# Pads of 96 instead of 64 columns around the sort buffers of a graph scatter kernel

## The chip, the cores and the metric

The kernel runs on one core of a Trainium2 chip. The metric is the device time of one execution in microseconds (us). Ten runs of the kernel before gave a median of 493.8 us, from 493.12 to 495.82.

## What is computed

There are N = 4096 nodes with 256 features each and E = 262144 edges, each with a source and a destination node. Every node gets its own features times `w_self`, and for each edge that ends in it the source's features times `w_msg`:

```python
self_out = nodes @ w_self
msg = nodes[edges_src] @ w_msg
agg = np.zeros((N, D)); np.add.at(agg, edges_dst, msg)
return self_out + agg
```

## The kernel before, in words

**Two stages.** The kernel first sorts the edges by a key made of the destination's segment, the source's block and the two low parts (lines 146 to 182), and then counts and multiplies. For a run of sorted edges that share a source block and a destination segment, TensorE adds up a matrix of edge counts with one-hot matrices (`onehots`, `count_mm`, lines 308 to 359), ScalarE copies it out of PSUM (`evac`), GpSimd's queue merges overlapping parts by DMA (`merge`), and TensorE multiplies it by Y = nodes @ w_msg (`apply_run`). This main loop begins at about 195 us. It takes its keys from the sort, so it can't begin before the sort is done. All instructions are issued in an order written out by hand (`tc.manual_schedule()`, line 98): on each engine they run in the order of the code.

**The sort's data.** The 262144 keys lie as 128 partitions by 2048 columns of f32. There are two such buffers, `XA[0]` and `XA[1]`, and each pass reads one and writes the other. Each buffer has `FP` columns in front of the keys, set to a very low value, and `BP` = 128 columns behind them, set to a very high one (lines 160 to 162). `FP` was 64.

**The sort's passes.** `SORT_A` (line 39) is a list of steps. `('b', h, par)` is a pass of compare-exchanges along the columns with gap h: VectorE writes the minimum of column c and column c + h to c, and the maximum to c + h, one instruction each (`mm`, line 591, with line 593 in the profile). Blocks of b columns, where b is the lowest set bit of h, are paired, and `par` says whether the even or the odd blocks are the lower ones. Each gap comes as two passes, par 0 and 1. `('q', bb, rots)` is a rotation: each group of columns is shifted across the partitions by its own number of rows. `rotate` (line 706) does it in two halves of 1024 columns. A half is 8 matmuls in the code (16 records in the trace) with a shifted identity, into two PSUM tiles, each copied out by ScalarE (line 719) into the other buffer. `('sh', ...)` is a shuffle on VectorE.

The part of the list around the change, after the gaps 962, 239, 376, 283 and 203:

```python
('b', 119, 0), ('b', 119, 1), ('b', 87, 0), ('b', 87, 1),
('q', 32, [...]), ('b', 78, 0), ('b', 78, 1), ('b', 30, 0), ('b', 30, 1), ('b', 42, 0), ('b', 42, 1),
('q', 16, [...]), ('b', 22, 0), ('b', 22, 1), ('b', 29, 0),
```

**Two ways to do a pass.** `run` (line 724) chooses by the gap. A gap above `FP` goes to `far_gap` (line 668), which does both passes of that gap in seven instructions and touches only columns that have a partner inside the keys; its first instruction reads nearly all columns. Gaps up to `FP` that follow each other are taken together by `near` (line 643). There a pass runs from -h to 2048, so that columns at the edges have a partner in the pads and nothing is left over. `near` can cut passes in two:

- *behind* a rotation (its argument `behind`): the first two passes start with the columns that depend on the first 1024 alone, as a first wave;
- *ahead* of a rotation (`ahead`): the last two passes are done first up to the columns that make the first 1024 complete, and then the rest, as a last wave. The cuts move with the gap and the block (lines 649 to 659).

`passes` (line 629) issues the waves one after the other. If a rotation is ahead, `near` also calls `warm` (line 597): ten matmuls of 512 zero columns, whose start is tied to an instruction of VectorE that lies at least 4.2 us (`PE_WARM_UP`) before the last wave, by an estimate of each instruction's length (columns / 960 + 0.1 us, line 589). `far_gap` calls no `warm`.

**After these steps** more groups of `near` and rotations follow, then a last rotation that is also a transpose (line 767) into `XS`, a pass list along the other direction (`SORT_S`), and between them `project` (line 220), which computes Y on TensorE and ScalarE; it needs `XT`, which the SP queue loads with 64 transposing DMAs (line 212).

## Time and profile before

| | |
|---|---|
| median of 10 runs | 493.8 us |
| the profiled execution's own time | 493.15 us |
| mean granted TensorE clock of the records | 0.915 |
| TensorE (PE) busy | 351.1 us, 71% |
| VectorE (DVE) busy | 446.3 us, 91% |
| ScalarE (ACT) busy | 239.3 us, 49% |
| GpSimd (POOL) busy | 158.3 us, 32% |
| passes on XA, line 593, all groups | 152 instructions |

The profile is of one execution. In the page's row by slices (40 equal ones, the busy share in tenths) the two stages can be told apart: VectorE is busy in nearly all of them up to the last two, TensorE fully only from the middle on.

```profile
PE   0000560575575006799999999999999999899995
DVE  8999399999889999999999999999999999989810
PEclk9999967799789556599999999999999999999999
```

A slice is 12.3 us. The 3 in the fifth slice of VectorE's row (49 to 61 us) is where the changed steps lie. PEclk is the granted clock of TensorE in tenths of full speed, as far as its records go. PE is the matmul side of TensorE and PEld the weight loads, L593 a line of the kernel; a matmul of f32 appears as two records. The table of waits names who waited, for whom, the us in total, how often, and the longest.

### The profile page before, as it was taken

To read this page: it belongs to the slowest core of one execution; us is meant where nothing else is said; L and a number is where in the kernel's file an instruction comes from. 1 tells how busy PE (TensorE), PEld (TensorE's weight loads), DVE (VectorE), ACT (ScalarE), POOL (GpSimd) and SP (SyncE) were. 2 spreads that over 40 slices of the span, in tenths; PEclk is the share of its full clock that TensorE was granted. 3 is DMA by queue.
4 is the path that set the end of the run, shared out by engine and by line. 5 is a ranking of instruction groups with operands and counts; after the bars stand their busy time and mean duration, and the time that the engine had idled before them with its cause. 6 is when DMAs were issued, how large, how long until landed. Compare 5 with 4: busy or idle time off the path is not lost.

```text
span 491.3 us, 10292 instructions
## 1 busy us (share of the span) xinstructions
PE 351.1 (71%) x4012; PEld 309.6 (63%) x4017; DVE 446.3 (91%) x411; ACT 239.3 (49%) x452; POOL 158.3 (32%) x154
## 2 busy tenths in 40 slices
PE   0000560575575006799999999999999999899995
PEld 0000530353452003699999999999999999799984
DVE  8999399999889999999999999999999999989810
ACT  3100110021155003457777777777777776677762
POOL 9100000000000000136455555555546454545640
PEclk9999967799789556599999999999999999999999
DMA  8971111111000000123333433344433343424341
GB/s 327 177 200 25 25 27 25 26 25 22 2 0 1 0 0 2 8 21 25 46 39 38 46 40 43 37 45 40 46 37 45 36 50 30 49 29 50 34 45 44
DMA packets 57756, 22.20 MB, mean 45 GB/s; under 512 B 43882, under 2 KB 56682, under 8 KB 57706
## 3 DMA queue, kind: packets, MB, share of 16 engines
q0 software_dynamic: 35920, 8.91, 21.6%
q1 hardware_dynamic: 21210, 10.52, 7.9%
q10 hardware_dynamic: 576, 2.10, 1.1%
q8 instruction: 33, 0.54, 0.5%
q14 instruction: 17, 0.14, 0.1%
HBM read 8.92 MB, written 6.30 MB: 31 GB/s over the span
## 4 chain that ended last, share of the span: by engine, by line
DVE 36%; PE 35%; issue 13%; POOL 13%; ACT 2%; DMA 1%; POOLq 0%; ACTq 0%; DVEq 0%
DVE XA L593 19%; PE ring L340 15%; PE out_ps L407 13%; POOL atr L384 13%; DVE XS L593 9%; PE tp_sw L715 4%; PE out_ps L402 2%; DVE e_oh L315 1%; DVE lo_c L123 1%; DVE d_oh L315 1%; PE out_ps L396 1%; DMA atr<-atr 1%; DVE XS L260 1%; ACT XA L719 1%; DVE XA L180 1%
## 5 line engine op out<-in xcount | busy, mean ns | idle before, releaser
L384 POOL DMA_DIRECT2D atr<-atr x130 | 145.2, 1180 | 318.3 <-ACT atr L364 315.0
L364 ACT CAST atr<-ring 128x486 bf16<-128x486 f32 x352 | 193.3, 567 | 85.7 <-PE ring L340 72.6
L340 PE MATMUL ring<-d_oh,e_oh 128*128 128x112 bf16 x2048 | 195.9, 215 | 7.8 <-DVE d_oh L315 5.0
L340 PEld LDWEIGHTS <-e_oh 128*128 128x128 bf16 x2048 | 166.9, 99 | 17.8 <-issue 7.0
L407 PE MATMUL out_ps<-Y,atr 128*128 128x256 bf16 x1056 | 170.0, 272 | 0.1
L315 DVE TENSOR_TENSOR e_oh<-slo_b,jrow 128x4096 bf16<-128x4096 int16 (+2 forms) x68 | 146.7, 2157 | 10.7 <-PE ring L340 10.3
L315 DVE TENSOR_TENSOR d_oh<-rel_b,jrow 128x3584 bf16<-128x3584 int16 (+2 forms) x68 | 129.5, 1904 | 0.0
L593 DVE TENSOR_TENSOR XA<-XA 128x510 f32<-128x510 f32 (+35 forms) x136 | 92.1, 722 | 12.8 <-ACT XA L719 11.1
L407 PEld LDWEIGHTS <-atr 128*128 128x128 bf16 x1056 | 92.1, 97 | 7.0 <-DMA atr<-atr 0.4
L340 PE MATMUL ring<-zer 128*128 128x224 bf16 x352 | 92.2, 262 | 0.9 <-ACT vals L265 0.7
L715 PE MATMUL tp_sw<-XA,id 128*128 128x128 f32 x192 | 28.2, 310 | 56.7 <-DVE XA L593 56.7
L605 PE MATMUL warm<-zw 128*128 128x512 bf16 x65 | 23.5, 524 | 62.4 <-DVE XA L593 32.6
L715 PEld LDWEIGHTS tp_sw<-XA,id 128*128 128x128 f32 x192 | 26.8, 222 | 60.1 <-issue 58.5
L719 ACT COPY XA<-tp_sw 128x512 f32<-128x512 f32 x24 | 14.2, 591 | 101.1 <-PE tp_sw L715 101.1
L605 PEld LDWEIGHTS <-zw 128*128 128x128 bf16 x70 | 8.2, 124 | 74.6 <-DVE XS L593 29.4
L593 DVE TENSOR_TENSOR XS<-XS 128x512 f32<-128x512 f32 (+17 forms) x40 | 46.0, 1196 | 2.6 <-ACT XS L771 2.0
L340 PEld LDWEIGHTS <-zer 128*128 128x128 bf16 x352 | 34.5, 98 | 1.3 <-ACT o_sb L416 0.5
L402 PE MATMUL out_ps<-Y,atr 128*128 128x256 bf16 x123 | 33.4, 271 | 0.1
L265 ACT CAST vals<-tp_sw 128x512 int16<-128x512 f32 x4 | 2.3, 585 | 36.2 <-PE tp_sw L264 36.2
L593 DVE TENSOR_TENSOR XA<-XA,XA 128x62 f32<-128x62 f32 (+7 forms) x16 | 14.7, 918 | 0.3
L224 PE MATMUL y_ps<-wcat,XT 128*128 128x256 bf16 x64 | 10.5, 270 | 3.3 <-ACT Y L228 3.3
L402 PEld LDWEIGHTS <-atr 128*128 128x128 bf16 x123 | 11.9, 96 | 0.3
(85 smaller groups left out, 113.9 us busy)
## 6 DMA issues: line engine op xcount, KB each, us to landing
atr<-atr POOLq DMA_DIRECT2D x98, 56.0 KB, 2.8
out_dram<-o_sb SPq DMA_DIRECT2D x110, 32.0 KB, 1.5
s<-in_edges_src_dram ACTq DMA_DIRECT2D x4, 512.0 KB, 9.3
d<-in_edges_dst_dram SPq DMA_DIRECT2D x4, 512.0 KB, 5.3
nodes_bf<-in_nodes_dram POOLq DMA_DIRECT2D x1, 2048.0 KB, 16.5
nodes_bf_dram<-nodes_bf SPq DMA_DIRECT2D x1, 2048.0 KB, 8.7
XT<-nodes_bf_dram SPq DMA_TRANSPOSE x64, 2.4
atr<-atr POOLq DMA_DIRECT2D x32, 28.0 KB, 2.8
```

Of the source, the lines that this page charges most:

```text
L123: nc.vector.tensor_scalar(out=out, in0=in_, scalar1=float(lo), scalar2=float(hi), op0=ALU.max, op1=ALU.min)
L224: nc.tensor.matmul(out=y_ps[:], lhsT=XT[:, k, t * P:(t + 1) * P], rhs=wcat[:, 2 + k, :], start=(k == 0), stop=(k == 1),)
L315: tt(out=o[:, 0:n // 2], in0=val[:, c:c + n].rearrange("p (g i) -> p g i", i=2).unsqueeze(2).to_broadcast(shp), in1=jrow[:, 0:wid, :].unsq ...
L340: mm = nc.tensor.matmul(out=ap, lhsT=lhsT, rhs=rhs, start=start, stop=True, skip_group_check=True,).ins
L364: ins = nc.scalar.copy(out=at[:, 0:SW + W], in_=ring[:, b:b + SW + W]).ins
L384: nc.gpsimd.dma_start(out=atr[:, b:b + n, 0:W], in_=atr[:, a:a + n, SW:SW + W], accum_op=ALU.add)
L402: nc.tensor.matmul(out=out_ps[:, 0, :], lhsT=spill[:, SW:SW + P], rhs=Y[:, b, :], start=False, stop=False, skip_group_check=True,)
L407: nc.tensor.matmul(out=out_ps[:, t, :], lhsT=at[:, t * P:(t + 1) * P], rhs=Y[:, b, :], start=False, stop=(b == NB - 1), skip_group_check=True,
L593: self.nc.vector.tensor_tensor(out=out, in0=in0, in1=in1, op=op),
L605: ins = self.nc.tensor.matmul(out=w[:], lhsT=self.zw[:, 0:P], rhs=self.zw[:], start=True, stop=True).ins
L715: self.nc.tensor.matmul(out=tp[:, g * P:(g + 1) * P], lhsT=self.turned(rots[8 * h + 4 * t + g]), rhs=sel(x)[:, 4 * t + g], start=True, sto ...
L719: self.nc.scalar.copy(out=sel(y)[:, 4 * t:4 * t + 4], in_=tp[:].rearrange("p (g i b) -> p g i b", g=4, b=bb),)
```

## The change

One constant: the pads in front of the sort buffers are 96 columns wide instead of 64, and since `run` compares the gaps with the same constant, gaps up to 96 are taken by `near` instead of `far_gap`.

```diff
-FP = 64
+FP = 96
 BP = 128
```

Nothing else is edited. The gaps of the list between 65 and 96 are 87 and 78, each with two passes. Gap 87 becomes a group of its own with a rotation ahead and none behind; gap 78 joins the group of 30 and 42, which thereby has a rotation behind it as well as ahead.

## Prediction

> **What bounds the kernel now.** I read the page first: its span, and the chain that ended last by engine.

> ```profile
> span 491.3 us, 10292 instructions
> DVE 36%; PE 35%; issue 13%; POOL 13%; ACT 2%; DMA 1%; POOLq 0%; ACTq 0%; DVEq 0%
> ```

> The chain changes hands once: VectorE (DVE) carries the sort, TensorE and the merges the main loop behind it. The change touches only the sort, so the second view is the table of who waited for whom, VectorE alone.

> ```profile
> DVE XA L593 <- ACT XA L719: 11.1, 6, 7.3
> DVE e_oh L315 <- PE ring L340: 10.3, 7, 3.8
> ```

> Six waits of the sort for the copy that ends a rotation (L719) sum to 11.1 us, and one of them alone is 7.3. The other row (one-hots waiting for TensorE) lies, by the timeline, wholly after 391 us; from 57 to 391 us VectorE has no gap over 2 us. So a microsecond that the sort saves starts the main loop a microsecond earlier, and nothing else that could set the end stands still: the transposing loads of XT end at 120 us and `project`, which needs them, starts at 141.7.

> Third, where the 7.3 us lies: the chain in order of time, 44.7 to 76 us (start, length, what).

> ```profile
> 44.78 1.20 DVE XA L593
> ...
> 49.62 6.75 PE tp_sw L715 x32
> ...
> 56.40 0.59 ACT XA L719
> ...
> 57.02 1.20 DVE XA L593
> ...
> 62.06 2.40 DVE XA L593 x2
> ...
> 66.92 1.40 DVE XA L593 x2
> 68.33 1.35 DVE XA L593 x2
> ...
> 69.82 2.04 PE tp_sw L715 x16
> ...
> 71.88 0.59 ACT XA L719
> ...
> 72.50 1.30 DVE XA L593 x2
> ```

> Two rotations stand side by side here. The first, `('q', 32, ...)`, lies between the gaps 87 and 78, which go through `far_gap`: VectorE ends gap 87 at 49.71, all 32 matmul records run with nothing beside them, and VectorE resumes at 57.02. The second, `('q', 16, ...)`, lies between groups that `near` cuts: the chain holds only the first half of the rotation (x16), VectorE's other waves run beside it, and its gap is 72.16 to 72.50, 0.34 us. The change makes the first look like the second.

> Last, the rows of the stretches, with busy time, count and clock (columns PE, PEld, DVE, ACT, POOL, PEclk, DMA share, GB/s).

> ```profile
> 49.71:57.01 7.30, 6.65 (x32) 6.46 (x32) 0.00 (x0) 2.34 (x4) 0.00 (x0) 1.00 0.12 27
> 69.70:72.17 2.47, 2.02 (x16) 1.86 (x16) 2.43 (x4) 0.87 (x2) 0.00 (x0) 1.00 0.12 27
> L715 PE MATMUL tp_sw<-XA,id x64: 275/275/551, 49.6 to 74.1; 128*128 128x128 f32 x64
> ```

> Half a rotation takes 3.3 us in the first row and 2.0 in the second, though both rows say clock 1.00. The third row (min, median, max ns of a matmul) tells why: 551 is twice 275, so the first rotation ran on a half clock; the record of the clock simply has no entry before it. No `warm` precedes that rotation, because only `near` with a rotation ahead calls it.

> **The change part by part.** With FP = 96 the test `op[1] <= FP` takes in the gaps 87 and 78 and no others.

> *Gap 87* becomes a `near` of two passes, cut ahead of the rotation. By L643-664 the cuts are 1112 and 1024: wave 1 has min/max pairs of 599 and 556 columns, wave 2 pairs of 468 and 512; 4270 columns in 8 instructions for 3922 in 7. Prices from rows of `near`: 1040 columns take 1239 ns and 554 take 734, so 1.04 ns a column; a pair of 1038 takes 62.06 to 64.49 = 2.42 us, which leaves 0.26 us a pair. Then 4270 x 1.04 ns + 4 x 0.26 = 5.48 us against 4.93 now (44.78 to 49.71): +0.55.

> *Gap 78* joins the group 30, 42, cut behind the rotation at 944 and 864: pairs of 510 and 472, then of 552 and 592; 4252 columns for 3940. 4252 x 1.04 ns + 4 x 0.26 = 5.46 against 5.04 now (57.02 to 62.06): +0.42. The later passes of the group keep their cuts.

> *The rotation.* Wave 1 of gap 87 takes 2310 x 1.04 ns + 0.52 = 2.92, by its nearest row (2176 columns in 66.92 to 69.68) 2.76 + 134 x 1.04 ns = 2.90; I take 2.90: it ends at 47.68. At the second rotation the way from there to VectorE's restart is 69.68 to 72.50 = 2.82 (semaphore, 16 matmuls, two copies). Restart: 50.50. Wave 2 fills 2.58 of it, so a gap of 0.24 stays of 7.31. VectorE then has 1964 columns of gap 78 that need only the first half: 1964 x 1.04 ns + 0.52 = 2.56 us. At the second rotation the last copy ended 2.45 after the restart (74.37 + 0.58 - 72.50), so the second half is hidden, with 0.1 us in hand; if that is missed, the cost is what the copy is late.

> The sum: next group at 47.68 + 2.82 + 5.46 = 55.96 instead of 62.06, a gain of 6.10 us. The same from the terms: 7.31 - 0.24 - 0.55 - 0.42 = 6.10. What is late next is VectorE itself, which has no gap before the next rotation.

> *The added `warm`.* Ten matmuls on a TensorE that is idle then; they wait for an instruction of VectorE, and behind them stands only the rotation. Counting back 4.2 us by L589's estimates from the end of wave 1 (556, 556, 599, 599, 59, 59, 905: 4.17; so one more 905: 5.21) ties them to the 60-column max of gap 119, done at 42.33; start 42.48, as at the next warm-up 0.15 after. There ten took 4.43 us at half clock; here they end by 46.9, before 47.83, when the rotation can start. They delay nothing; whether they do their work is the open cost.

> [...] Row first: at the next warm-up, 64.60 to 69.03, the rows of one microsecond show the clock at 0.50 up to 69.0 and 0.79 in 69 to 70, so it rose at 69.42; it had fallen at 59.18 (0.59 in 59 to 60), 10.24 earlier. [...] I take the row: gain 6.1. [...]

> [...] Now one of them starts cold (VectorE's gap at 126.5 us is 1.94 instead of about 0.35) the others are warm. Bounds: all warm -1.6; one more fully cold +2.6. I take 0. [...]

> *Pads.* The memsets of 96 columns instead of 64 lie at 1.4 to 1.8 us on POOL; the 64-column one takes 0.17 us, so two of them cost under 0.2 us together on a queue whose nodes arrive long before use. VectorE's first dependent work is far later. Nothing. No DMA is added or moved.

> **The rivals.**

> *Cold rotation, or one later rotation cold.* Gain 3.5 to 4.4: 489.4 to 490.3. For: the 1.94 gap shows that a warm-up can miss. Against: four others did not.

> *The split does not happen* because a wait ties the first half to wave 2 (or the first wave of 78 to the whole rotation). Then +0.97 of passes stays, and a warm rotation (2.65 + 2.5 for 7.31) saves about 2.2: 492.6. Against: gap 9, with the same block of 1, is cut before a rotation at 95 us and that one starts beside wave 2.

> [...]

> **How the numbers follow.** The profiled execution took 493.15 us, its span 491.3; minus 6.1 gives 487.05 and 485.2. The median of the runs is 493.8, 0.65 above the profiled one; with it 487.7. Chances: the full gain 0.62 (486 to 488.7, with moved windows); cold rotation 0.26 (489.4 to 490.3); no split 0.06; slower by the clock 0.04; gain lost to within the noise 0.02. Range 486.0 to 490.6. Under 0.2% (1 us) a measurement can't tell from no change: faster 0.94, same 0.02, slower 0.04.

> **What would show it.** In the profile after: VectorE's wait for L719 falls from 11.1 to about 4, and no gap of 7 us is left; a `warm` group starts near 42.5; the first rotation's 16 matmuls start near 47.8, beside 468- and 512-column passes, at 275 ns each; 510-column passes start near 50.5; the 1038-column pair near 56.0. [...] If the first rotation is as said and the time still isn't 6 lower, the gaps of the later rotations have grown. The prediction fails if the rotation starts only when the 512s are done.

## The result, and the profile after

The changed kernel took 487.76 us (median of 15 runs, 484.67 to 493.29), beside 493.87 us for the kernel before (52 runs): ratio 0.9874, 95% interval 0.9855 to 0.9894, a gain of 5.2 to 7.2 us. The runs furthest above their kernel's fastest are left out of ratios. The profiled execution took 488.82 us with a span of 486.9, 4.4 below that of before, so this one profile shows less than the median.

Who waited for whom, VectorE, in the changed kernel (us in total, times, longest):

```profile
DVE e_oh L315 <- PE ring L340: 8.1, 7, 3.1
DVE XA L593 <- ACT XA L719: 8.0, 6, 2.1
```

The 7.3 us wait is gone, but the sum fell only from 11.1 to 8.0. The chain in order of time around the first rotation, same kernel (start, length, what):

```profile
46.25 1.40 DVE XA L593 x2
...
47.69 3.79 PE tp_sw L715 x16
...
51.51 0.59 ACT XA L719
...
52.13 1.30 DVE XA L593 x2
...
57.48 2.40 DVE XA L593 x2
```

The chain now holds only half a rotation (x16), started at 47.69 beside wave 2: both cuts work. But the half took 3.79 us where 2.0 was forecast; VectorE resumed at 52.13, not 50.50, and the 1038-column pair started at 57.48, not 55.96. The matmuls say why (min, median, max ns, between 46 and 76 us):

```profile
L715 PE MATMUL tp_sw<-XA,id x64: 275/421/579, 47.7 to 70.5; 128*128 128x128 f32 x64
```

A median of 421 between 275 and 551 means that about half of the records ran on a half clock. The `warm` was there, ten matmuls from 42.57 (forecast 42.48), and did not lift the clock in time. The rows of one microsecond (busy time and count of PE, PEld, DVE, ACT, POOL, then PEclk, DMA share, GB/s) show when it rose:

```profile
50.00:51.00 1.00, 1.00 (x6) 1.00 (x6) 0.08 (x1) 0.39 (x1) 0.00 (x0) 1.00 0.15 33
51.00:52.00 1.00, 1.00 (x8) 1.00 (x7) 0.00 (x0) 0.49 (x1) 0.00 (x0) 1.00 0.14 33
52.00:53.00 1.00, 1.00 (x12) 1.00 (x11) 0.87 (x2) 0.49 (x2) 0.00 (x0) 1.00 0.10 20
```

PEclk says 1.00 throughout only because the record's first entry is a rise at 51.77; the counts, 6 matmuls a microsecond and then 12, show the change. Two later rotations were cold as well: VectorE's gaps at 67.6 and 94.5 us are 2.06 and 2.03, where before they were 0.34 and 0.30.

### The profile page after: what moved, and what is told of

Its sections match the earlier page's. It is cut to its first block, busy times and chain, and to the rows that moved or that the text cites. A ratio compares the mean times of both kernels' runs of the same rounds, so it can differ in the third digit from the quotient of the medians.

```text
span 486.9 us, 10312 instructions
## 1 busy us (share of the span) xinstructions
PE 357.0 (73%) x4022; PEld 313.9 (64%) x4027; DVE 447.1 (92%) x413; ACT 239.5 (49%) x452; POOL 158.4 (33%) x154
## 4 chain that ended last, share of the span: by engine, by line
PE 52%; DVE 33%; issue 4%; DMA 3%; POOL 3%; ACT 3%; SPq 0%; ACTq 0%; POOLq 0%; DVEq 0%
PE ring L340 23%; PE out_ps L407 20%; DVE XA L593 18%; DVE XS L593 9%; PE tp_sw L715 4%; POOL atr L384 3%; PE out_ps L402 2%; DMA d<-in_edges_dst_dram 2%; PE out_ps L396 2%; DVE e_oh L315 1%; DVE d_oh L315 1%; DMA atr<-atr 1%; ACT atr L364 1%; DVE XS L260 1%; ACT XA L719 1%
## 5 line engine op out<-in xcount | busy, mean ns | idle before, releaser
L340 PE MATMUL ring<-d_oh,e_oh 128*128 128x112 bf16 x2048 | 195.6, 215 | 6.7 <-DVE d_oh L315 5.3
L340 PEld LDWEIGHTS <-e_oh 128*128 128x128 bf16 x2048 | 166.5, 98 | 16.0 <-issue 5.4
L315 DVE TENSOR_TENSOR e_oh<-slo_b,jrow 128x4096 bf16<-128x4096 int16 (+2 forms) x68 | 146.7, 2158 | 8.4 <-PE ring L340 8.1
L315 DVE TENSOR_TENSOR d_oh<-rel_b,jrow 128x3584 bf16<-128x3584 int16 (+2 forms) x68 | 129.6, 1905 | 0.0
L593 DVE TENSOR_TENSOR XA<-XA 128x510 f32<-128x510 f32 (+35 forms) x142 | 97.1, 731 | 9.7 <-ACT XA L719 8.0
L605 PE MATMUL warm<-zw 128*128 128x512 bf16 x75 | 28.1, 537 | 102.9 <-DVE XA L593 72.9
L340 PE MATMUL ring<-zer 128*128 128x224 bf16 x352 | 91.8, 261 | 0.7 <-ACT vals L265 0.7
L605 PEld LDWEIGHTS <-zw 128*128 128x128 bf16 x80 | 9.4, 125 | 117.1 <-issue 53.6
L719 ACT COPY XA<-tp_sw 128x512 f32<-128x512 f32 x24 | 14.2, 592 | 99.7 <-PE tp_sw L715 99.7
L593 DVE TENSOR_TENSOR XS<-XS 128x512 f32<-128x512 f32 (+17 forms) x40 | 46.0, 1197 | 2.9 <-ACT XS L771 2.4
L715 PEld LDWEIGHTS tp_sw<-XA,id 128*128 128x128 f32 x192 | 29.3, 241 | 12.0 <-issue 9.0
L715 PE MATMUL tp_sw<-XA,id 128*128 128x128 f32 x192 | 30.5, 328 | 8.2 <-DVE XA L593 8.2
L340 PEld LDWEIGHTS <-zer 128*128 128x128 bf16 x352 | 34.4, 98 | 1.2 <-ACT o_sb L416 0.5
L228 ACT CAST Y<-y_ps 128x256 bf16<-128x256 f32 x32 | 10.5, 378 | 2.8 <-PE y_ps L224 2.8
```

Of the source, the lines that this page charges most:

```text
L228: nc.scalar.copy(out=Y[:, t, :], in_=y_ps[:])
L315: tt(out=o[:, 0:n // 2], in0=val[:, c:c + n].rearrange("p (g i) -> p g i", i=2).unsqueeze(2).to_broadcast(shp), in1=jrow[:, 0:wid, :].unsq ...
L340: mm = nc.tensor.matmul(out=ap, lhsT=lhsT, rhs=rhs, start=start, stop=True, skip_group_check=True,).ins
L593: self.nc.vector.tensor_tensor(out=out, in0=in0, in1=in1, op=op),
L605: ins = self.nc.tensor.matmul(out=w[:], lhsT=self.zw[:, 0:P], rhs=self.zw[:], start=True, stop=True).ins
L715: self.nc.tensor.matmul(out=tp[:, g * P:(g + 1) * P], lhsT=self.turned(rots[8 * h + 4 * t + g]), rhs=sel(x)[:, 4 * t + g], start=True, sto ...
```

## The experiments

Three theories were put to the test. The sum of terms of the prediction (6.1 us at full clock) is common to all; they differ on the warm-up. In the profiles of before and of the change the granted clock changes 14 times each, and all changes of one profile lie whole multiples of 3.413 us apart. Below, a window is such a stretch of 3.413 us, it is filled as far as TensorE has matmuls in it, and its place in an execution is its phase. **P**: the phase differs from execution to execution, and the clock rises at the end of a window filled to a bit over 80% (88% did it in the profile of before, at 69.42, and 79% did not in that of the change, at 48.36); ten matmuls (4.43 us at half clock) fill one of two windows so far unless a window ends 1.6 to 2.8 us after their start, so they do it in about two phases of three (an estimate). **W**: ten matmuls do it always (what the prediction took). **S**: it takes a window filled wholly, which ten matmuls give in (4.43 - 3.41)/3.41, three phases of ten (an estimate too).

What a cold rotation costs the three take from the profile of before. There the first half of the first rotation took 4.37 us from its first matmul to the end of its second copy (49.62 to 53.99), and that of the second rotation, which was warm, 2.65 (69.82 to 72.47): 1.72 less. The cold one's copies started 1.71 us apart (51.70, 53.41, 55.12), so a cold second half comes 3.42 us behind the first, 0.86 more than the 2.56 us of passes beside it (an estimate). As a yardstick I use, beside the times, the start of the first 1038-column pair (gap 30), which comes right behind all that the change touches; below it is called the pair. In the kernel before it is 62.06.

**No warm-up**, both cuts kept:

```diff
-        if ahead:
+        if ahead and ps[0][0] != 87:
             self.warm(marks[-2])
```

> The change with both cuts, but without the new warm-up before the first rotation. Theory P (a warm-up lifts the clock only if a window of 3.41 us is filled to over some 80% in time, which happens in about two of three phases): here the first half is always on half clock, VectorE's gap is about 2.0 us and the second half may be up to 0.9 late, so 489.5 to 490.4, some 1.2 us above the changed kernel's mean, and less spread than it. Rival W (ten matmuls always do it): 489.5 to 490.4 too, but then a full 1.7 to 2.6 above the changed kernel. Rival S (a whole window is needed, so the rotation is cold in 70% of the phases anyway): no more than 0.6 above the changed kernel.

Measured 491.3 us (7 runs), ratio to before 0.9925 (0.9896 to 0.9955), a gain of 2.2 to 5.2 us; the forecast was 3.5 to 4.4. The cuts are worth that much without a warm-up. The three theories are not told apart by this run: the changed kernel's own ratios, 0.9874 above and 0.9901 and 0.9843 below, lie 1.2 to 4.1 us under it, so the differences of 1 to 2 us that they forecast are lost in this. In its profile VectorE waits 2.11 us for the first half and, since the clock rose only at 53.83, another 0.39 for the second. So the chain shows the whole cold rotation in a row; the pair starts at 58.05:

```profile
47.80 6.70 PE tp_sw L715 x32
...
54.52 0.59 ACT XA L719
...
55.14 1.39 DVE XA L593 x2
```

**Only the cut ahead:** gap 87 in `near`, gap 78 in `far_gap`.

```diff
-            if op[0] == "b" and op[1] <= FP:
+            if op[0] == "b" and op[1] <= FP and op[1] != 78:
...
-                while e < len(ops) and ops[e][0] == "b" and ops[e][1] <= FP:
+                while e < len(ops) and ops[e][0] == "b" and ops[e][1] <= FP and ops[e][1] != 78:
```

> Gap 87 goes to near (cut ahead, with its warm-up), gap 78 stays in far_gap. VectorE must wait for the whole rotation: gap about 0.24 + 2.45 = 2.7 us where warm, 4.4 where the first half is cold. By the sum of terms 7.31 - 2.7 - 0.55 = 4.1 us gained where warm (489.8), 2.4 where cold (491.5); theory P 490.3 on average.

Measured 490.3 us, ratio 0.9895 (0.9863 to 0.9928), a gain of 3.6 to 6.8 us; the kernel before took 495.21 beside it, so the agreement with 490.3 is chance, and the 3.6 us that P forecast on average lie at the interval's edge. In its profile VectorE's gap at the first rotation was 2.76 us (2.7 worked out for a warm one), and the pair started at 57.82, 4.24 before 62.06 (worked out: 4.1). Its chain waits for the second half alone:

```profile
50.14 2.06 PE tp_sw L715 x16
...
52.23 0.59 ACT XA L719
...
52.85 1.20 DVE XA L593
```

**Only the cut behind:** the same edit with 87 in place of 78.

> Gap 78 goes to near (cut behind), gap 87 stays in far_gap, so no warm-up and no cut ahead. VectorE waits for the first half, on half clock: gap 4.4 us; the second half lies behind 2.56 us of passes and is up to 0.9 late. Gain 7.31 - 4.4 - 0.42 - (0 to 0.9) = 1.6 to 2.5: 491.4 to 492.3. With the part cut ahead this sums to about the whole; if the two need each other, this one gives less than 1.

Measured 493.09 us, ratio 0.9942 (0.9923 to 0.9962), a gain of 1.9 to 3.8. VectorE resumes after a cold half, and the pair starts at 59.54, 2.52 before 62.06; the second half was not late, because the clock rose at 53.73 on the rotation's own matmuls. By the pair, the two parts sum to 6.8, and the whole change gains 6.3 with a warm rotation (below) and 4.6 with a cold one.

```profile
49.72 3.77 PE tp_sw L715 x16
...
53.52 0.59 ACT XA L719
```

**Only a warm-up**, in the kernel before:

```diff
             elif op[0] == "q":
+                if op[1] == 32:
+                    self.warm(len(self.log))
                 self.rotate(x, y, *op[1:])
```

> The kernel before, with nothing but a warm-up of ten matmuls put before the first rotation. Warm, the rotation from its first matmul to its last copy takes about 4.5 us (as the one at 101.6 us, whose two halves run back to back) for 7.3: gain 2.7 where warm. Theory W: 491.2. Theory P, two of three phases: 492.1. Theory S, three of ten: 493.1.

Measured 492.63 us, ratio 0.9947 (0.9924 to 0.997): a gain of 1.5 to 3.8. In its profile the rotation's 32 records took 3.85 us on the chain instead of 6.75, and VectorE's gap was 4.32 instead of 7.31. The mechanism is as forecast; the interval holds the values of P and W, and S lies below it.

**Pads alone** (FP = 96, but both tests of `run` read `op[1] <= 64`):

> Pads of 96 columns, but near still takes gaps up to 64 only, so the passes are those of the kernel before. All theories: no change, 493.9 within 0.6, first rotation's gap about 7.

Measured 494.13 against 494.2, ratio 0.9996 (0.9974 to 1.0018). The wider memset takes 0.18 us where the narrower took 0.17; no cost of the pads can be seen. The rotation's gap was 6.57 for 7.31 in the profile of before: without any warm-up it too went with the clock's rise (at 54.26 here, at 55.77 there).

**The change again**, unedited, in three more profiles:

> The changed kernel once more, unedited, for a second profile and as the reference of the three beside it. Theory P: the windows of the clock lie elsewhere in its profile, and so other rotations, or none, show the 2.0 us gap; the times scatter over some 8 us again. Theory W and S with a fixed phase: the same rotations cold as in the first profile, at the same offsets.

Measured 489.74 us (6 runs, 488.81 to 492.36), ratio 0.9901 (0.9873 to 0.9929). What P was said to show here did not come: the times scatter over 3.6 us, and the same three rotations are cold as in the first profile, because the windows lay within 0.2 us of where they lay there. A fixed phase would show the same; the third profile, with another phase, rules it out.

> The changed kernel unedited, a third look, with times beside the next one. Theory P, with the threshold the profiles so far bracket (a window with matmuls in 80% of it did not lift the clock, one with 83% did): the first rotation is cold if a window ends 1.63 to 2.80 us after the warm-up's start (42.57), that is a third of the phases, then its gap is 2.05 and the 1038-column pair starts at 57.5; otherwise the gap is about 0.3 and the pair starts at 55.8.

Measured 486.56 us (6 runs, 485.27 to 488.86), ratio 0.9843 (0.9804 to 0.9882). Here the rotation is warm.

> A fourth look at the changed kernel. The same rule by the phase of its own windows: pair at 57.5 for a window end 1.63 to 2.80 us after 42.57, else at 55.8.

One time alone, 491.07. With the first profile and the version cut ahead only, these are five profiles of the same warm-up. The end of the first window after its start is worked out from the clock's changes in steps of 3.413 us:

| profile | warm-up from | window ends after | rule of P | first rotation's gap | pair at |
|---|---|---|---|---|---|
| changed, first | 42.57 | 2.37 | cold | 2.05 | 57.48 |
| changed, second | 42.58 | 2.18 | cold | 2.04 | 57.49 |
| changed, fourth | 42.57 | 2.52 | cold | 2.05 | 57.50 |
| changed, third | 42.59 | 3.23 | warm | 0.32 | 55.78 |
| cut ahead only | 42.57 | 0.43 | warm | (2.76) | (57.82) |

All five agree with P. W is out (three are cold). S is out too: in the third profile of the change the clock rose at 45.82, and the window that ended there had matmuls in 94% of it, not in all.

P's numbers don't hold as they stand, though. The profiles of all versions hold thirty warm-ups of ten matmuls that begin on half clock ahead of a rotation on XA. In 13 of them the window ended 1.78 to 2.52 us after the start, and the rotation was cold; in 17 it ended up to 1.41 or from 2.66 us after it, and the rotation was warm. Two of the warm ones (2.66 and 2.74, pads alone) lie where the rule of 1.63 to 2.80 says cold. Here is the first of them, by the window that ended at 91.81 and the next one (columns as in the rows above): 2.67 of 3.41 us, 78%, were enough.

```profile
88.39:91.81 3.42, 2.67 (x7) 1.02 (x8) 3.35 (x4) 0.00 (x0) 0.00 (x0) 0.50 0.13 29
91.81:95.22 3.41, 1.85 (x13) 1.14 (x12) 3.38 (x6) 0.00 (x0) 0.00 (x0) 1.00 0.12 27
```

The 83% of the rule came from a burst with nine of its ten records in the trace, and so was too low. By the thirty, the cold range is 0.74 to 1.25 us wide, which I estimate as 22 to 37% of the phases if all are equally likely; that they are is not shown.

In the third profile of the change the sum of the prediction can be read as it was meant; its chain:

```profile
47.72 2.06 PE tp_sw L715 x16
...
49.81 0.59 ACT XA L719
...
50.42 1.30 DVE XA L593 x2
...
55.78 2.40 DVE XA L593 x2
```

Forecast were 47.83, 50.50 and 55.96; measured 47.72, 50.42 and 55.78, a gain of 6.28 for 6.10. Its waits, against "about 4":

```profile
DVE XA L593 <- ACT XA L719: 3.5, 7, 0.9
```

The same profiles suggest why the changed kernel's times scatter more (standard deviation 2.6 us over its 15 runs, 1.3 over the 52 of before). A cold rotation delays what follows by 1.7 us (57.48 against 55.78), half a window. In the first profile the next two warm-ups start 17.4 and 44.4 us after the first (59.93 and 86.97), 5.1 and 13.0 windows, and so meet the windows at about the same cold place; all three rotations are cold in each of the three cold profiles. In the warm one the next ones start at 58.23 and 83.55, 4.6 and 12.0 windows after the first, and all three are warm. The first one-hot, which comes right behind the sort, is at 193.26, 193.15 and 193.40 in the cold profiles and at 188.49 in the warm one, 4.8 us apart in the same program. Before, it was at 195.23. In order: before, the change's first profile, its third:

```profile
195.23 0.69 DVE L315 TENSOR_TENSOR e_oh<-slo_b,jrow 128x1024 bf16<-128x1024 int16 x1
193.26 0.69 DVE L315 TENSOR_TENSOR e_oh<-slo_b,jrow 128x1024 bf16<-128x1024 int16 x1
188.49 0.69 DVE L315 TENSOR_TENSOR e_oh<-slo_b,jrow 128x1024 bf16<-128x1024 int16 x1
```

**Longer warm-ups**, in the changed kernel and in the kernel before:

```diff
+        free = sum(t for _, t in self.log[self.rot:ready])
+        lead, count = (7.0, 16) if free > 12.0 else (PE_WARM_UP, 10)
         i, t = ready, 0.0
-        while t < PE_WARM_UP:
+        while t < lead:
...
-        for k in range(10):
+        for k in range(count):
```

> The changed kernel with warm-ups of 16 matmuls tied 7.0 us ahead, wherever over 12 us of passes lie since the last rotation; the others stay at ten and 4.2. 16 matmuls at half clock take 6.8 us, two windows, so a whole window is filled in every phase. Theory P: no rotation behind a long warm-up is cold, gaps about 0.3, a mean 2 to 3 us below the changed kernel (about 485) and a spread less than half of its. Theory W: no change. Theory S: 5 to 6 us below.

Measured 488.09 us, ratio to before 0.9876 (0.9851 to 0.9902), beside 0.9901 for the change measured next to it: not told apart, so the forecast 2 to 3 us are not shown, nor is a spread of less than half (3.5 us here, 3.6 there). Its profile is as P says: gaps of 0.31, 0.34 and 0.30 at the first three rotations, the pair at 55.77, the first one-hot at 188.40. But the third profile of the change shows the same without longer warm-ups.

> The kernel before with the same long warm-ups, none before its first rotation. Theory P: the later rotations are always warm, about 1.5 to 2 us below the kernel before (492.1), first gap unchanged near 7; and the long-warm version of the changed kernel stays over 6 us below this one, since its first rotation is always warm. Theory W: 493.9.

Measured 494.39, ratio 0.9991 (0.9965 to 1.0017): a miss, as the 1.5 to 2 us did not come. The two rotations behind long warm-ups were warm (gaps 0.34 and 0.30), but two behind short ones had gaps of 1.71 and 1.43, and the main loop, from the first one-hot to the last matmul, took 293.8 us for 290.3 in the profile of before. The longer warm-ups of the changed kernel did stay over 6 us below this one, as forecast (488.09).

The third version is the same edit on the changed kernel with 14 matmuls, a lead of 6.0 and a limit of 7.0:

> The changed kernel with warm-ups of 14 matmuls tied 6.0 us ahead wherever over 7 us of passes lie since the last rotation, so before the later short groups too. Theory P: 14 matmuls are 6.0 us at half clock, enough to fill a window to over 83% in any phase; no gap over 1 us before a rotation is left, 2 to 3 us below the changed kernel beside it, 486 to 487.5. Rival: the later rotations' matmuls are held up by the longer warm-ups, gaps of 0.5 to 1 grow there and nothing is gained over the version with 16.

Measured 488.52 us (6 runs), ratio 0.9868 (0.9834 to 0.9903): a miss too, no better than the change beside it (486.56). The profile names one reason. TensorE's matmuls in 104 to 128 us, in order of time, with the idle time before them in brackets:

```profile
111.65 3.19 PE L608 MATMUL warm<-zw 128*128 128x512 bf16 x13 [0.15 <-DVE XA L594]
118.93 6.39 PE L720 MATMUL tp_sw<-XA,id 128*128 128x128 f32 x32 [4.08 <-DVE XA L594]
```

This warm-up met a clock that was already full, was through in 3.19 us instead of 6, and left 4.08 us idle; the window 114.11 to 117.52 had matmuls in 22% of it, the clock fell, and the rotation at 118.93 began cold (VectorE's gap 2.08). Here a warm-up counted in matmuls was too short because the clock was up.

## Why the prediction was right, point by point

**The place and the mechanism** were right: the one long wait was the uncut rotation, and both cuts took effect. The cut ahead alone moved the pair by 4.24 us (4.1 worked out), the cut behind alone by 2.52 (1.6 to 2.5).

**The passes' price** was right: the first wave of gap 87 ended at 47.65 in the changed profile (forecast 47.68), and gap 78, from VectorE's restart at 52.13 to the pair at 57.48, took 5.35 (5.46). The cover of the second half by the first wave of gap 78 held in the cold profiles too. The 3.5 forecast for a cold rotation has in it a second half that comes 0.86 late, and no run shows that: the clock rose during the rotation's own matmuls (at 51.77 in the first profile), without a warm-up the second half came 0.39 late, and cold, the pair gained 4.6.

**"I take the row: gain 6.1"** was the open step, and it holds for some phases only. The row is one warm-up of the kernel before: a window ended 1.41 us after its start (64.60), the next was filled to 88%, and the clock rose at its end, 69.42. That a window filled so far lifts the clock held (94% did in the third profile of the change). That the added warm-up meets the windows as well was not shown, and it differs: in the first profile after, a window ended 2.37 us after its start, the two that it lay in were filled to 70 and 79%, and the rotation was cold. So the row should have been turned into a share of phases. By P it is about two thirds, by the thirty warm-ups 63 to 78% (estimates, both with all phases equally likely); the text gave the full gain a chance of 0.62, but without that working.

**"I take 0", for the later rotations,** was mis-sized. Before, one of them was cold (VectorE's gap at 126.5 us, 1.94). No run shows the 2.6 us for one more cold rotation; one that turned cold raised VectorE's gap by 1.7 (2.06 and 2.03 for 0.34 and 0.30). In the cold profiles two later rotations turned cold, about +3.4 us. So the first one-hot of the first profile came only 1.97 us earlier (195.23 to 193.26); in the warm profile it came 6.74 earlier. The median of 487.76 beside a forecast of 487.7 lies among what these kinds of execution give, and its closeness is partly luck: the three blocks of runs of this kernel had medians of 487.8, 489.7 and 486.6.

**"Nothing else that could set the end stands still"** was right of the order, but the main loop is not of fixed length. From the first one-hot to the start of the last matmul it took 290.3 us in the profile of before and, in the order of the profiles of the change, 288.0, 291.5, 289.6 and 290.1; over all versions 288.0 to 293.8. The clock's rise in the loop is not the cause between the first two: it came 12.1 and 12.0 us after the first one-hot. The loop's length follows neither the sort's end nor the kernel. In the first profile after, 2.4 of the 4.4 us of span come from it. TensorE's waits for the merges' DMAs and for issue differ between these profiles (240 to 460 us: 0.3 and 0.8 us in the first of the change, 1.0 and 1.1 in the second), but what sets them was not tried, and this stays open. So does why the runs of one block lie together (all six of the second block at 488.8 or above, all six of the third at 488.9 or below; the two ran on different chips, where the kernel before took 494.2 and 494.72), and whether a lasting gain from surer warm-ups is hidden under this scatter.

## What to carry to other kernels

Where one wait is twenty times its neighbour of the same kind, search for the structural difference between the two places: here a constant chosen for padding also decided which passes could be cut beside a rotation. Price such a change at both clocks of TensorE (half a rotation took 3.79 us in the first profile of this change and 2.06 in the third), since whether a short warm-up works was here a matter of its phase. Where total times scatter by as much as the effect, compare the start of one fixed instruction behind the change, in several profiles: the first profile of this change showed 4.4 us of span, a later one of the same program 7.5.
